# Attention scores of a half head: three passes over 64 rows from unstacked queries and keys, in place of two passes over 128 rows from stacked ones

## The chip, the cores and the metric

The kernel runs on one core of one Trainium2 chip. The metric is the time of one execution on the device in microseconds (us). The kernel before took 1044.98 us, the median of three runs (1044.03 to 1045.5). All inputs and outputs lie in the chip's memory as float32.

## The reference, cut to what matters

One layer over 512 tokens of width 2048, with 16 learned meta tokens ahead of them (528 rows). A normalised input is multiplied by one matrix of 2048 x 8192. Its columns are the queries, keys, values and gates of 8 heads of retention and of 8 heads of differential attention, 128 columns a head each. A head of the attention has two half heads of 64 columns, with a softmax each. The outputs of all heads are normalised, gated and multiplied by a second matrix of 2048 x 2048, added to the input and normalised once more.

```python
def diff_attention(q, k, v, valid, lam):          # q, k: (B, L, H, 2, 64), v: (B, L, H, 128)
    ...
        s = jnp.einsum('bqhcd,bkhcd->bhcqk', qb, k).astype(jnp.float32) * scale
        s = jnp.where(allowed[None, None, None], s + bias[None, :, None], -jnp.inf)
        p = jax.nn.softmax(s, axis=-1)
        a = p[:, :, 0] - lam * p[:, :, 1]
        return jnp.einsum('bhqk,bkhe->bqhe', a.astype(v.dtype), v)
```

The change touches how `s` is computed: for each half head `c`, the product of a block of 128 queries with the keys they may see, a sum over 64 numbers.

## The kernel before, in words

The kernel keeps float32 accuracy on a matrix engine that takes a shorter format (`F32R` in the code): each operand is split into a high part, rounded to that format, and a low part, the rest. A product of two such operands is then three products: high by high, high by low, low by high. The fourth, low by low, is left out.

The program goes through the 8 heads. For each, `project` makes eight projections one after the other (`rv rq rk rg dv dq dk dg`; in the last head the four of the attention come first). A projection is 16 blocks of 128 rows of the contraction times three products, so 48 products of 512 columns, or 96 of 264 columns where the 16 meta tokens are needed too (names ending in `v` and `k`). Its weights come from memory in pieces of 512 KB. ScalarE rounds each piece (`wh`, line 104) and VectorE subtracts (`wl`, line 105).

The attention and retention of a head are generators, `ret_task` and `diff_task`. They are advanced by `step` between the pieces of the projections, so that their small products stand among the next projections' large ones. The exact place of each instruction on its engine is set by the tile framework's scheduler, which simulates a time line while the program is built and orders each engine's queue by it; engines then run their queues in that order.

The steps that the change touches, all for one head `h` of the attention:

- After projection `dq` (lines 712 to 722) the queries, 128 partitions by 512 tokens in PSUM, are written to SBUF. Half head `s` holds partitions 64 s to 64 s + 63. Before, each half head gets its own tile of 128 partitions, the high part in the upper 64 and the low part in the lower 64: one ScalarE and one VectorE instruction a half head.
- After projection `dk` (lines 723 to 735) each half head's keys are written as two tiles of 128 partitions, [high; high] and [low; low]. For each half head and each of the two PSUM tiles of 264 columns these are two ScalarE and two VectorE instructions over 64 partitions.
- In `diff_task` (lines 555 to 597) there are four blocks of 128 queries, `b` = 0 to 3, which see 144, 272, 400 and 528 keys. For each half head the scores are two products over 128 rows: [q high; q low] by [k high; k high], and by [k low; k low]. (This includes low by low.) For `b` = 3 the 528 keys are two parts of 264 columns, so four products. The scores sit in PSUM tiles `s_d`: three buffers shared with other small products (`pm`) for `b` < 3, one double buffer (`pd`) for `b` = 3. VectorE adds the distance term and takes the row's maximum (line 584), ScalarE takes the exponential (line 587). The two softmaxes are combined, transposed (line 608) and multiplied by the values.

A stacked operand uses all 128 rows of the matrix engine though the contraction has only 64.

Of the kernel before, what the change touches and what calls it, by code (L numbers as in the profile page):

```python
# [28 lines left out]
# |o| beyond OMAX squares past float32. Squares are of o / 2; QMAX is the mean of 128 of them at which  # L29
# the sum of o * o passes float32 (its 1/sqrt is then 0)  # L30
# [6 lines left out]
def hymba_kernel(ctx: ExitStack, tc: tile.TileContext, x, meta, norm_g, w_in, w_out, g_ret, g_diff,  # L37
# [12 lines left out]
    def f(t):  # L50
        return t.bitcast(F32)
# [10 lines left out]
    # ---------------- weight pieces: 1024 columns of a partition at a time, split into hi and lo  # L62
    # in the last head the attention goes before the retention, whose way to the output is shorter
# [12 lines left out]
    for n0, nw in chunks:  # L76
        n = 1024 // nw
        # the last head's two outputs come last
        for ks in pairs if n0 == 0 else [slice(k, k + n) for k in range(0, KT, n)]:
            pieces.append((w_out_t[:, ks, n0:n0 + nw], nw))  # L80
# [6 lines left out]
    def load_raw(upto):  # L87
        for i in range(len(raws), min(upto, len(pieces))):
            src, nw = pieces[i]
            if i == 3:  # L90
                # one more buffer than the others have: the gates' of the attention
                raws[i] = [ap.tile([P, SEQ], F32, tag=t, name=f"wr{i}_{t}") for t in ("sgr", "sgd")]
                for j, r in enumerate(raws[i]):
                    nc.sync.dma_start(out=r.rearrange("p (k n) -> p k n", n=nw),
                                      in_=src[:, j * 4:j * 4 + 4, :])
                continue
            r = wp.tile([P, 1024], F32, tag="wr", name=f"wr{i}")
            nc.sync.dma_start(out=r.rearrange("p (k n) -> p k n", n=nw), in_=src)
            raws[i] = [r[:, :512], r[:, 512:]]
            if i >= 4:  # L100
                raws[i] = [r]
# [5 lines left out]
    def place(i):  # L107
        """Buffers of a piece's hi and lo, in as many parts as it is split in."""
        nw = pieces[i][1]
        if i < 2 or i == len(pieces) - 4:  # L110
            # the first projection's pieces, and one of the last four, sit in buffers of the attention
            parts = [(ap.tile([P, 512], F32R, tag="r2k", bufs=4, name=f"wh{i}_{j}"),
                      ap.tile([P, 512], F32R, tag=("vh", "vl")[i % 2], bufs=2, name=f"wl{i}_{j}")) for j in range(2)]
        elif i == 2:
            parts = [[ap.tile([P, L], F32R, tag=f"{t}{j}", name=f"w{i}_{t}{j}")[:, :512] for t in ("dkh", "dkl")]
                     for j in range(2)]
        else:
            hi, lo = (wp.tile([P, 1024], F32R, tag=t, name=f"{t}{i}") for t in ("wh", "wl"))
            n = 1024 // len(raws[i])
            parts = [(hi[:, j:j + n], lo[:, j:j + n]) for j in range(0, 1024, n)]  # L120
        kp = 1024 // nw // len(parts)
        views = [[t.rearrange("p (k n) -> p k n", n=nw) for t in p] for p in parts]
        loaded[i] = lambda k: [t[:, k % kp, :] for t in views[k // kp]]
        return parts
# [17 lines left out]
    # ---------------- inputs, constants  # L142
    xt = big.tile([P, 4, D], F32, tag="mix", name="xt")
    # the meta tokens' rows in quarters: partition 16 q + t holds columns 512 q .. of row t
# [31 lines left out]
    # adds the four quarters of each row of the meta tokens  # L176
# [3 lines left out]
    # ---------------- u = rms_norm(h) transposed, split  # L180
# [3 lines left out]
    def rsqrt_rows(r, n, nm):  # L184
        """r: sums of D squares per row -> 1/sqrt(mean + EPS)."""
        pool.tensor_scalar(r[:n], r[:n], 1.0 / D, EPS, op0=ALU.mult, op1=ALU.add)
        pool.tensor_tensor(out=r[:n], in0=r[:n], in1=mhalf[:n, 0:1], op=ALU.pow)
# [5 lines left out]
    def row_squares(j, c0, c1, eng):  # L193
        """Sums of squares of some columns of 128 tokens."""
        t = xt[:, j, c0 * P:c1 * P]
        jk = ap.tile([P, 1024], BF16, tag=("p2", "p2", "dq0", "dq1")[j], bufs=2 if j < 2 else 1, name=f"jk_x{j}_{c0}")[:, :(c1 - c0) * P]
        to = parts_x[j][:, used[j]:used[j] + 1]
        used[j] += 1
        if eng is act:
            act.activation(jk, t, AF.Square, accum_out=to)  # L200
        else:
            vec.tensor_tensor_reduce(jk, t, t, op0=ALU.mult, op1=ALU.add, scale=1.0, scalar=0.0, accum_out=to)
# [18 lines left out]
    def warm(n):  # L221
        """The tensor engine's clock rises only under load: keep it busy until there is work."""
# [32 lines left out]
    def turn(i, s, j):  # L255
        """Two 128-column blocks of 128 tokens' rows, transposed."""
# [27 lines left out]
    def first_two():  # L284
        """The first value and query projections, in step with the arrival of the tokens and the weights."""
# [8 lines left out]
        def run(i, half, s, which):  # L294
            """Products of two blocks of 128 of a projection's contraction."""
# [114 lines left out]
    # lambda: exp(lq1.lk1) - exp(lq2.lk2) + lam_init, negated, on every partition  # L410
# [12 lines left out]
    # tiles of 16 keys go through the tensor engine once: [hi; hi; lo] against [hi; lo; hi], 32 partitions apart  # L423
# [13 lines left out]
    # ---------------- attention tasks; each yield lets projection products go in between  # L437
    mix = {"f": big.tile([P, 2 * HEADS, SEQ], F32, tag="mix", name="mixf")}

    def finish(po, col, T, gate, nm):  # L440
        oc = ap.tile([P, L], F32, tag="s2k", bufs=4, name=f"oc_{nm}")[:, :SEQ]
        vec.tensor_scalar(oc, po, OMAX, -OMAX, op0=ALU.min, op1=ALU.max)
        # squares of both halves of the partitions summed, then [hi; lo] of them over the partitions
# [9 lines left out]
        # mean squares along one row -> over the partitions -> 1/sqrt -> back along a row, on every partition  # L453
# [20 lines left out]
    def v_rows(vT, nm, centre):  # L474
# [4 lines left out]
        # retention: key tiles of 128 from the first meta token, 16 keys last  # L479
        # attention: the meta tokens' tile last, then full tiles of tokens  # L480
# [74 lines left out]
    def diff_task(h, T):  # L555
# [3 lines left out]
        qs = T["dq"]  # L559
        ks = T["dk"]  # L560
        aa = []
        for b in range(4):
            w = 2 * 72 + P * b
            zz = sm.tile([P, 2], F32, tag="zz", name=f"zz_{nm}_{b}")
            pp = []
            for s in range(2):
                if b < 3:
                    sp = pm(f"s_{nm}_{b}_{s}")[:, :w]
                    for i in range(2):
                        pe.matmul(sp, qs[s][:, b * P:(b + 1) * P], ks[s][i][:, :w], start=i == 0, stop=i == 1)  # L570
                    shape = lambda t: t
                else:
                    sp = pd(f"s_{nm}_{b}_{s}")[:, :, :HL]
                    for i in range(2):
                        for q in range(2):
                            pe.matmul(sp[:, q, :], qs[s][:, b * P:(b + 1) * P], ks[s][i][:, q * HL:(q + 1) * HL],  # L576
                                      start=i == 0, stop=i == 1)
# [20 lines left out]
        # A transposed: (rows, key column, first query, columns) per tile; the products follow one step behind  # L598
# [31 lines left out]
    # ---------------- projections  # L630
# [42 lines left out]
    def early_mix():  # L673
        """The first heads' outputs, split while the last projection runs."""
# [6 lines left out]
    for h in range(HEADS):  # L681
        T = {}
        for name in order[h]:
# [28 lines left out]
            elif name == "dq":  # L712
                # each half head's queries as [hi; lo] over the partitions, scaled by powers of two
                (o, a, b), = outs
                c = DH ** -0.5 * 2.0 ** (h + 1)
                T[name] = []
                for s in range(2):
                    t = ap.tile([P, SEQ], F32R, tag=f"dq{s}", name=f"{nm}_{s}")
                    src = o[s * DH:(s + 1) * DH]
                    act.activation(t[:DH], src, AF.Copy, scale=c)  # L720
                    vec.scalar_tensor_tensor(t[DH:], src, c, f(t[:DH]), op0=ALU.mult, op1=ALU.subtract)
                    T[name].append(t)
            else:
                # each half head's keys as [hi; hi] and [lo; lo]
                T[name] = []
                for s in range(2):
                    t1 = ap.tile([P, L], F32R, tag=f"dkh{s}", name=f"{nm}h_{s}")
                    t2 = ap.tile([P, L], F32R, tag=f"dkl{s}", name=f"{nm}l_{s}")
                    for o, a, b in outs:
                        src = o[s * DH:(s + 1) * DH]  # L730
                        act.copy(out=t1[:DH, a:b], in_=src)
                        act.copy(out=t1[DH:, a:b], in_=src)
                        vec.tensor_tensor(out=t2[:DH, a:b], in0=src, in1=f(t1[:DH, a:b]), op=ALU.subtract)
                        vec.tensor_tensor(out=t2[DH:, a:b], in0=src, in1=f(t1[DH:, a:b]), op=ALU.subtract)
                    T[name].append((t1, t2))
# [8 lines left out]
    # ---------------- output projection, residual, final norm  # L744
# [13 lines left out]
    for ci, (n0, nw) in enumerate(chunks):  # L758
# [21 lines left out]
        def evac(t):  # L780
            # rows so far, their squares' sums, and the rows times the final gain
# [36 lines left out]
        else:  # L818
            prefetch(pi + np_)
            wt = [loaded.pop(pi + i) for i in range(np_)]  # L820
            for t in range(4):
# [6 lines left out]
                # the last rows in more parts: nothing else is left for their way out to hide behind  # L828
# [11 lines left out]
def tables():  # L840
    """Constants of the shapes: -|q - k| with the chunk mask, and each head's decay g ** |t - s| with its mask."""
# [55 lines left out]
```

## Time and profile before

| | |
|---|---|
| Median of three runs | 1044.98 us |
| Profiled execution, first to last instruction (span) | 1049.9 us |
| TensorE: matmul busy, share, instructions | 1029.7 us, 98%, 6423 |
| TensorE: weight loads busy | 926.3 us, 88% |
| VectorE busy | 511.4 us, 49% |
| ScalarE busy | 448.1 us, 43% |
| Mean granted TensorE clock | 0.993 |

The profile is one execution, whose span is 4.9 us above the median of the timed runs. PE is the matmul side of TensorE, PEld its weight loads, DVE is VectorE, ACT ScalarE, POOL GpSimd, SP the engine whose queue issues most DMAs. Matmuls are pipelined, so the duration of one is its way through the array; what it costs in a row of matmuls is the distance from its start to the next one's start, called its slot here. A weight load normally starts as the matmul before it starts.

### The profile page before, as it was taken

Reading aid. Unit: us, or ns where it says so; the run is one execution under the profiler, and the core shown is the slowest. Engines: PE = TensorE matmul, PEld = TensorE weight load, DVE = VectorE, ACT = ScalarE, POOL = GpSimd, SP = SyncE. Lnnn points to the kernel's source line nnn. Section 1 sums busy time; section 2 is a strip of 40 time slices with the busy share of each in tenths; the row PEclk is TensorE's granted clock in tenths of the full one; section 3 lists DMA queues with packets and bytes.
Section 4 is the critical chain, followed back from the end, with each engine's and each line's share of the span. In section 5 each row is a group of like instructions: output and inputs, shape, how many; then the busy total and the mean of one; then the engine's idle time right before and its main releaser. Section 6 shows DMA issues by size and latency. Waiting matters only on the chain.

```text
span 1049.9 us, 15748 instructions
## 1 busy us (share of the span) xinstructions
PE 1029.7 (98%) x6423; PEld 926.3 (88%) x6423; DVE 511.4 (49%) x1012; ACT 448.1 (43%) x814; POOL 48.0 (5%) x96
## 2 busy tenths in 40 slices
PE   6999999999999999999999999999999999899996
PEld 6999998999899989998999899989899888788896
DVE  6553544454445444645463536353637462344342
ACT  6443544363436343634363436343636452232232
POOL 3200000000000000000000000000000000000001
PEclk8999999999999999999999999999999999999999
DMA  9323332342233223322433233323332314373324
GB/s 282 92 83 102 93 87 81 83 110 82 81 87 107 81 81 96 97 83 79 102 91 93 68 103 90 101 61 103 91 101 69 103 61 130 92 261 100 101 61 160
DMA packets 156312, 105.70 MB, mean 101 GB/s; under 512 B 8320, under 2 KB 143632, under 8 KB 155728
## 3 DMA queue, kind: packets, MB, share of 16 engines
q1 hardware_dynamic: 155632, 102.86, 34.1%
q10 hardware_dynamic: 576, 1.84, 0.5%
q8 instruction: 50, 0.82, 0.3%
q14 instruction: 22, 0.18, 0.1%
q0 software_dynamic: 32, 0.01, 0.0%
HBM read 100.43 MB, written 4.23 MB: 100 GB/s over the span
## 4 chain that ended last, share of the span: by engine, by line
PE 94%; DMA 3%; ACT 1%; DVE 1%; POOL 1%; issue 0%; SPq 0%; POOLq 0%
PE pj_dv L282 9%; PE pj_rk L282 9%; PE pj_dk L282 9%; PE pj_rv L282 9%; PE pj_dg L282 9%; PE pj_dq L282 9%; PE pj_rg L282 9%; PE pj_rq L282 9%; PE y L511 5%; PE y L509 4%; PE y L510 4%; PE s_d L570 1%; PE at_d L608 1%; PE s_d L576 1%; DMA xt<-in_x_dram 1%; PE ut L262 1%
## 5 line engine op out<-in xcount | busy, mean ns | idle before, releaser
L104 ACT CAST wh<-wr 128x1024 fp32r<-128x1024 f32 (+1 forms) x157 | 163.2, 1041 | 321.7 <-issue 117.4
L105 DVE TENSOR_TENSOR wl<-wr,wh 128x1024 fp32r<-128x1024 f32 (+1 forms) x157 | 190.8, 1217 | 218.8 <-ACT wh L104 218.2
L509 PE MATMUL y<-wh,mh 128*128 128x512 f32 (+1 forms) x260 | 90.4, 349 | 2.8 <-ACT mh L670 2.8
L511 PE MATMUL y<-wh,ml 128*128 128x512 f32 (+1 forms) x260 | 90.8, 351 | 0.0
L510 PE MATMUL y<-wl,mh 128*128 128x512 f32 (+1 forms) x260 | 90.7, 349 | 0.0
L509 PEld LDWEIGHTS y<-wh,mh 128*128 128x128 f32 x260 | 49.6, 191 | 9.4 <-ACT mh L670 3.2
L282 PE MATMUL pj_rk<-uh,wh 128*128 128x264 f32 x256 | 56.3, 288 | 0.0
L282 PE MATMUL pj_rk<-uh,wl 128*128 128x264 f32 x256 | 55.6, 285 | 0.0
L282 PE MATMUL pj_rk<-ul,wh 128*128 128x264 f32 x256 | 55.5, 284 | 0.0
L511 PEld LDWEIGHTS y<-wh,ml 128*128 128x128 f32 x260 | 49.7, 191 | 6.2
L510 PEld LDWEIGHTS y<-wl,mh 128*128 128x128 f32 x260 | 49.5, 191 | 6.1
L282 PE MATMUL pj_dv<-uh,wh 128*128 128x264 f32 x256 | 54.3, 286 | 0.0
L587 ACT ACTIVATE p_d<-p_d,mx_d 128x144 f32<-128x144 f32 (+3 forms) x64 | 36.6, 572 | 40.5 <-DVE mx_d L586 39.3
L282 PE MATMUL pj_rv<-uh,wh 128*128 128x264 f32 x256 | 53.3, 287 | 0.3
L282 PE MATMUL pj_rv<-uh,wl 128*128 128x264 f32 x256 | 53.3, 286 | 0.0
L282 PE MATMUL pj_rv<-ul,wh 128*128 128x264 f32 x256 | 52.8, 285 | 0.0
L282 PE MATMUL pj_dv<-uh,wl 128*128 128x264 f32 x256 | 52.6, 286 | 0.0
L282 PE MATMUL pj_dk<-uh,wh 128*128 128x264 f32 x256 | 52.3, 286 | 0.0
L282 PE MATMUL pj_dv<-ul,wh 128*128 128x264 f32 x256 | 52.1, 285 | 0.0
L282 PE MATMUL pj_dk<-uh,wl 128*128 128x264 f32 x256 | 52.0, 285 | 0.0
L282 PE MATMUL pj_dk<-ul,wh 128*128 128x264 f32 x256 | 51.9, 284 | 0.0
L282 PE MATMUL pj_dq<-uh,wh 128*128 128x512 f32 x128 | 51.2, 400 | 0.0
(402 smaller groups left out, 2445.9 us busy)
## 6 DMA issues: line engine op xcount, KB each, us to landing
wr<-in_w_in_dram SPq DMA_DIRECT2D x127, 512.0 KB, 4.2
wr<-in_w_out_dram SPq DMA_DIRECT2D x32, 512.0 KB, 3.9
xt<-in_x_dram SPq DMA_DIRECT2D x8, 512.0 KB, 7.0
hr<-in_x_dram SPq DMA_DIRECT2D x4, 1024.0 KB, 8.3
tab<-in_decay_tab_dram SPq DMA_DIRECT2D x8, 288.0 KB, 2.8
bc_r<-rd_r SPq DMA_DIRECT2D x8, 256.0 KB, 4.1
bc_d<-rd_d SPq DMA_DIRECT2D x8, 256.0 KB, 4.6
out_dram<-hr ACTq DMA_DIRECT2D x4, 448.0 KB, 3.8
```

The source lines that it names most:

```text
L104: act.copy(out=hi, in_=raw)
L105: eng.tensor_tensor(out=lo, in0=raw, in1=f(hi), op=ALU.subtract)
L262: pe.transpose(groups[i, s][:, k, j * P:(j + 1) * P], xt[:, 2 * i + j, c * P:(c + 1) * P], ident)
L282: pe.matmul(o, w_, u_[:, kt, a:b], start=first, stop=last)
L509: pe.matmul(o, ah, bh, start=start, stop=False)
L510: pe.matmul(o, ah, bl, start=False, stop=False)
L511: pe.matmul(o, al, bh, start=False, stop=stop)
L570: pe.matmul(sp, qs[s][:, b * P:(b + 1) * P], ks[s][i][:, :w], start=i == 0, stop=i == 1)
L576: pe.matmul(sp[:, q, :], qs[s][:, b * P:(b + 1) * P], ks[s][i][:, q * HL:(q + 1) * HL], start=i == 0, stop=i == 1)
L587: act.activation(p, p, AF.Exp, bias=mx, scale=slope, accum_out=zz[:, s:s + 1])
L608: pe.transpose(at[:n, b * P - q0:(b + 1) * P - q0], aa[b][:, kc:kc + n], ident)
```

## The change

The queries and keys are no longer stacked. `dq` is written as one high and one low tile of 128 partitions by 512, `dk` as one high and one low tile of 128 by 528; half head 0 is partitions 0 to 63 of each, half head 1 partitions 64 to 127. A half head's scores are three products over its own 64 partitions (high by high, high by low, low by high) instead of two over 128. The program marks such a product as one for half of the array's rows, the first half for half head 0, the second for half head 1. For `b` < 3 the code asks for both half heads' products in turn, one of each; for `b` = 3 it asks for the six products of one half head and then, after a `yield`, for the six of the other.

```diff
-        qs = T["dq"]
-        ks = T["dk"]
...
+            def operands(s):
+
+                rows = slice(s * DH, s * DH + DH)
+                qh, ql = (t[rows, b * P:(b + 1) * P] for t in T["dq"])
+                kh, kl = (t[rows] for t in T["dk"])
+                return (qh, kh), (qh, kl), (ql, kh)
+
+            if b < 3:
+                sps = [pm(f"s_{nm}_{b}_{s}")[:, :w] for s in range(2)]
+                for i in range(3):
+                    for s in range(2):
+                        q_, k_ = operands(s)[i]
+                        pe.matmul(sps[s], q_, k_[:, :w], start=i == 0, stop=i == 2)
             for s in range(2):
                 if b < 3:
-                    sp = pm(f"s_{nm}_{b}_{s}")[:, :w]
-                    for i in range(2):
-                        pe.matmul(sp, qs[s][:, b * P:(b + 1) * P], ks[s][i][:, :w], start=i == 0, stop=i == 1)
+                    sp = sps[s]
                     shape = lambda t: t
                 else:
                     sp = pd(f"s_{nm}_{b}_{s}")[:, :, :HL]
-                    for i in range(2):
-                        for q in range(2):
-                            pe.matmul(sp[:, q, :], qs[s][:, b * P:(b + 1) * P], ks[s][i][:, q * HL:(q + 1) * HL],
-                                      start=i == 0, stop=i == 1)
+                    for q in range(2):
+                        for i, (q_, k_) in enumerate(operands(s)):
+                            pe.matmul(sp[:, q, :], q_, k_[:, q * HL:(q + 1) * HL], start=i == 0, stop=i == 2)
...
                 (o, a, b), = outs
                 c = DH ** -0.5 * 2.0 ** (h + 1)
-                T[name] = []
-                for s in range(2):
-                    t = ap.tile([P, SEQ], F32R, tag=f"dq{s}", name=f"{nm}_{s}")
-                    src = o[s * DH:(s + 1) * DH]
-                    act.activation(t[:DH], src, AF.Copy, scale=c)
-                    vec.scalar_tensor_tensor(t[DH:], src, c, f(t[:DH]), op0=ALU.mult, op1=ALU.subtract)
-                    T[name].append(t)
+                hi, lo = (ap.tile([P, SEQ], F32R, tag=f"dq{i}", name=f"{nm}_{i}") for i in range(2))
+                act.activation(hi, o, AF.Copy, scale=c)
+                vec.scalar_tensor_tensor(lo, o, c, f(hi), op0=ALU.mult, op1=ALU.subtract)
+                T[name] = (hi, lo)
             else:
-                T[name] = []
-                for s in range(2):
-                    t1 = ap.tile([P, L], F32R, tag=f"dkh{s}", name=f"{nm}h_{s}")
-                    t2 = ap.tile([P, L], F32R, tag=f"dkl{s}", name=f"{nm}l_{s}")
-                    for o, a, b in outs:
-                        src = o[s * DH:(s + 1) * DH]
-                        act.copy(out=t1[:DH, a:b], in_=src)
-                        act.copy(out=t1[DH:, a:b], in_=src)
-                        vec.tensor_tensor(out=t2[:DH, a:b], in0=src, in1=f(t1[:DH, a:b]), op=ALU.subtract)
-                        vec.tensor_tensor(out=t2[DH:, a:b], in0=src, in1=f(t1[DH:, a:b]), op=ALU.subtract)
-                    T[name].append((t1, t2))
+                hi, lo = (ap.tile([P, L], F32R, tag=f"dk{t}0", name=f"{nm}{t}") for t in "hl")
+                for o, a, b in outs:
+                    act.copy(out=hi[:, a:b], in_=o)
+                    vec.tensor_tensor(out=lo[:, a:b], in0=o, in1=f(hi[:, a:b]), op=ALU.subtract)
+                T[name] = (hi, lo)
```

Lines after the change stand about 10 further down in `diff_task`: the score products are lines 577 and 586 (570 and 576 before). The rows of the built programs below have the scheduler's order. `s_d_1_0` is the score tile of block `b` = 1, half head 0. Before, `dq_0` and `dq_1` are the stacked queries of half heads 0 and 1; after, `dq_0` is the high tile of both half heads and `dq_1` the low one. Numbers at the ends of names count buffers.

PE in head 0, blocks 0 and 1, among the products of projection `dg`, before:

```order
L570 MATMUL s_d_0_0_1257<-dk0l_1213,dq_0_1083 128x144
L282 MATMUL pj_dg_0_1278<-uh,wl_1161 128x512
L282 MATMUL pj_dg_0_1278<-uh,wh_1160 128x512
L570 MATMUL s_d_0_1_1265<-dk0h_1222,dq_1_1086 128x144
L570 MATMUL s_d_1_0_1312<-dk0h_1212,dq_0_1083 128x272
L282 MATMUL pj_dg_0_1278<-ul,wh_1160 128x512
L570 MATMUL s_d_1_0_1312<-dk0l_1213,dq_0_1083 128x272
```

and after:

```order
L577 MATMUL s_d_0_0_1241<-dk0h,dq_0_1083 128x144
L577 MATMUL s_d_0_1_1242<-dk0h,dq_0_1083 128x144
L282 MATMUL pj_dg_0_1264<-ul,wh_1101 128x512
L282 MATMUL pj_dg_0_1264<-uh,wl_1102 128x512
L577 MATMUL s_d_1_0_1298<-dk0h,dq_0_1083 128x272
L282 MATMUL pj_dg_0_1264<-uh,wh_1158 128x512
L577 MATMUL s_d_0_0_1241<-dk0l,dq_0_1083 128x144
L577 MATMUL s_d_0_1_1242<-dk0l,dq_0_1083 128x144
L577 MATMUL s_d_0_0_1241<-dk0h,dq_1_1084 128x144
L577 MATMUL s_d_0_1_1242<-dk0h,dq_1_1084 128x144
L577 MATMUL s_d_1_0_1298<-dk0l,dq_0_1083 128x272
L577 MATMUL s_d_1_0_1298<-dk0h,dq_1_1084 128x272
```

The six products of block 0 now stand as three pairs, one product of each half head; block 1's first half head stands unpaired, and products over 128 rows (`pj_dg`) come between.

PE in head 0, block 2, before:

```order
L282 MATMUL pj_rv_0_1387<-uh,wl_1282 128x264
L570 MATMUL s_d_2_0_1366<-dk0h_1212,dq_0_1083 128x400
L570 MATMUL s_d_2_0_1366<-dk0l_1213,dq_0_1083 128x400
L570 MATMUL s_d_2_1_1374<-dk0h_1222,dq_1_1086 128x400
L570 MATMUL s_d_2_1_1374<-dk0l_1223,dq_1_1086 128x400
L282 MATMUL pj_rv_1_1388<-uh,wl_1282 128x264
```

and after:

```order
L577 MATMUL s_d_2_0_1354<-dk0h,dq_0_1083 128x400
L577 MATMUL s_d_2_1_1355<-dk0h,dq_0_1083 128x400
L577 MATMUL s_d_2_0_1354<-dk0l,dq_0_1083 128x400
L577 MATMUL s_d_2_1_1355<-dk0l,dq_0_1083 128x400
L577 MATMUL s_d_2_0_1354<-dk0h,dq_1_1084 128x400
L577 MATMUL s_d_2_1_1355<-dk0h,dq_1_1084 128x400
```

Four products of one kind became three pairs with nothing between them. Block 3 is, in each half head, a row of six products of that half head (four before).

DVE in head 0, from the first key instruction to the first score instruction, before:

```order
L733 TENSOR_TENSOR dk0l_0_1213<-pj_dk0_0_1099,dk0h_0_1212 64x264
L734 TENSOR_TENSOR dk0l_0_1213<-pj_dk0_0_1099,dk0h_0_1212 64x264
L471 TENSOR_TENSOR oc_r0_1089<-oc_r0_1089,bc_r0_1241 128x512
L733 TENSOR_TENSOR dk0l_0_1213<-pj_dk0_1_1100,dk0h_0_1212 64x264
L734 TENSOR_TENSOR dk0l_0_1213<-pj_dk0_1_1100,dk0h_0_1212 64x264
L501 TENSOR_TENSOR vl_d0_1245<-vp_d0_1243,vh_d0_1244 128x512
L472 SCALAR_TENSOR_TENSOR mixf_625<-oc_r0_1089,gcol_94,sg_rg0_860 128x512
L733 TENSOR_TENSOR dk0l_1_1223<-pj_dk0_0_1099,dk0h_1_1222 64x264
L734 TENSOR_TENSOR dk0l_1_1223<-pj_dk0_0_1099,dk0h_1_1222 64x264
L733 TENSOR_TENSOR dk0l_1_1223<-pj_dk0_1_1100,dk0h_1_1222 64x264
L734 TENSOR_TENSOR dk0l_1_1223<-pj_dk0_1_1100,dk0h_1_1222 64x264
L505 TENSOR_TENSOR v_std_618<-vp_d0_1243,v_std_618 16x128
```

and after:

```order
L733 TENSOR_TENSOR dk0l_1211<-pj_dk0_0_1097,dk0h_1210 128x264
L733 TENSOR_TENSOR dk0l_1211<-pj_dk0_1_1098,dk0h_1210 128x264
L471 TENSOR_TENSOR oc_r0_1087<-oc_r0_1087,bc_r0_1225 128x512
L501 TENSOR_TENSOR vl_d0_1229<-vp_d0_1227,vh_d0_1228 128x512
L472 SCALAR_TENSOR_TENSOR mixf_625<-oc_r0_1087,gcol_94,sg_rg0_860 128x512
L505 TENSOR_TENSOR v_std_618<-vp_d0_1227,v_std_618 16x128
```

All the low keys are now made ahead of line 471, which waits for a DMA; before, three quarters of them stood behind it.

## Rows read from the trace of the kernel before

**Rows 1.** The page: busy time by engine, the granted clock, the chain.

```profile
PE 1029.7 (98%) x6423; PEld 926.3 (88%) x6423; DVE 511.4 (49%) x1012; ACT 448.1 (43%) x814; POOL 48.0 (5%) x96
...
PEclk8999999999999999999999999999999999999999
...
PE 94%; DMA 3%; ACT 1%; DVE 1%; POOL 1%; issue 0%; SPq 0%; POOLq 0%
```

**Rows 2.** Waits of PE, the one behind start-up: line, waited for, us, times, longest.

```profile
PE y L509 <- ACT mh L670: 2.8, 1, 2.8
```

**Rows 3.** Time line of PE: start, duration, instruction; a product of 144 columns.

```profile
117.64 0.40 PE L282 MATMUL pj_dg<-ul,wh 128*128 128x512 f32 x1
117.87 0.23 PE L570 MATMUL s_d<-dk0h,dq 128*128 128x144 f32 x1
...
118.22 0.39 PE L282 MATMUL pj_dg<-uh,wh 128*128 128x512 f32 x1
```

**Rows 4.** Time line of PE: products of 400 and 264 columns.

```profile
125.96 0.34 PE L570 MATMUL s_d<-dk0h,dq 128*128 128x400 f32 x1
...
126.68 0.28 PE L282 MATMUL pj_rv<-uh,wl 128*128 128x264 f32 x1
...
131.18 0.41 PE L576 MATMUL s_d<-dk0h,dq 128*128 128x264 f32 x2
...
131.67 0.28 PE L282 MATMUL pj_rv<-uh,wh 128*128 128x264 f32 x1
```

**Rows 5.** Time line of PE and PEld, from 64-row products to 128-row ones, start-up.

```profile
6.84 0.19 PE L234 MATMUL first<-part_m,sel 64*64 64x1 f32 x1
6.97 0.14 PEld L224 LDWEIGHTS idle<-ident 128*128 128x128 f32 x1
7.13 0.38 PE L224 MATMUL idle<-ident 128*128 128x128 f32 x2
...
11.07 0.53 PE L242 MATMUL first<-ident,mt 64*128 64x64 f32 x3
11.29 0.31 PE L242 MATMUL first<-ident,mt 64*128 64x64 f32 x1
11.53 0.29 PEld L224 LDWEIGHTS idle<-ident 128*128 128x128 f32 x2
11.80 0.64 PE L224 MATMUL idle<-ident 128*128 128x128 f32 x2
12.02 0.63 PE L224 MATMUL idle<-ident 128*128 128x128 f32 x2
```

**Rows 6.** Stretches of the same start-up; the clock stands after POOL's column.

```profile
5.50:8.80 3.30, 0.96 (x7) 0.50 (x5) 0.84 (x3) 1.05 (x2) 0.74 (x2) 1.00 0.93 323
9.00:15.00 6.00, 4.09 (x20) 3.83 (x21) 3.30 (x10) 4.99 (x9) 1.67 (x4) 0.50 1.05 291
```

**Rows 7.** Time line of PE and PEld: weights of 16 columns between ones of 128.

```profile
143.35 0.39 PE L282 MATMUL pj_rq<-uh,wl 128*128 128x512 f32 x1
143.35 0.42 PEld L608 LDWEIGHTS at_d<-ident,p_d 128*16 128x16 f32 x3
143.58 0.49 PE L608 MATMUL at_d<-ident,p_d 128*16 128x128 f32 x3
144.14 0.40 PE L282 MATMUL pj_rq<-ul,wh 128*128 128x512 f32 x1
```

**Rows 8.** Key and query instructions of ACT and DVE, 96 to 125 us.

```profile
L731 ACT CAST dk0h<-pj_dk 64x264 fp32r<-64x264 f32 x4 | 1.5, 373 | 3.6 <-DVE dk0l L734 3.4
L720 ACT ACTIVATE dq<-pj_dq 64x512 fp32r<-64x512 f32 x2 | 1.2, 586 | 1.5 <-DVE dq L721 1.5
L500 ACT CAST vh_d<-vp_d 128x512 fp32r<-128x512 f32 x1 | 0.6, 587 | 0.0
L734 DVE TENSOR_TENSOR dk0l<-pj_dk,dk0h 64x264 fp32r<-64x264 f32 x4 | 1.7, 431 | 0.1
```

**Rows 9.** Who waited for line 734, the low keys: us in total, times.

```profile
  PEld s_d L570: 1.4, 4
```

## The prediction

> **What bounds the kernel now.** First the page: PE is busy for 1029.7 of 1049.9 us and the chain that ends last is 94% PE, with the granted clock high almost throughout; DVE and ACT are under half busy [rows 1]. Then the waits of PE: behind the start-up there is one of note, 2.8 us near the end [rows 2]. So time is the number of PE's instructions times the distance from one start to the next (a slot), and I read slots from the time line.
>
> Three slots matter. A product of 512 columns takes 0.23 us (117.64 to 117.87). One of 144 columns and one of 512 behind it take 0.35 together (117.87 to 118.22), so the short one costs 0.12, though its columns alone would be 144/512 of 0.23, or 0.065 [rows 3]. I take 0.116 for it, and read it as a floor: what the load of the next 128-column weights takes. Products of 400 columns take 0.18 (four in 0.72), those of 264 take 0.122 (four in 0.49) [rows 4]; 272 columns lie just above, 0.125.
>
> **The score products, taken as a plain row.** Before, a head has four products each of 144, 272 and 400 columns and eight of 264: 4 x 0.116 + 4 x 0.125 + 4 x 0.18 + 8 x 0.122 = 2.66 us. The change makes six, six, six and twelve of them with the same columns, half as many again: +1.33 a head, +10.6 us over eight. Half the rows do not make a product shorter: at start-up the 64-row products of 64 columns stand 0.11 apart and the 128-row ones of 128 columns 0.21 (11.07 to 11.29 is two slots, 11.80 to 12.02 one) [rows 5], so columns set the slot.
>
> **What pairs give back.** Where two half heads stand next to each other, the two halves of the array could work at once. The order has this for block 0 and block 2 of seven heads, three pairs each. In the last head no two neighbours are of different halves; blocks 1 and 3 have no such pairs anywhere, and block 3 alone holds twelve of a head's thirty products. No row shows two such products. From one side: nothing overlaps, +10.6. From the other: a pair takes one product's slot, weights included, so blocks 0 and 2 save 3 x 0.116 + 3 x 0.18 = 0.89 us a head, 6.2 over seven heads, and +4.4 is left. I take the middle course that the floor suggests: the streams overlap but the weight loads, one a product, still follow each other at 0.116. Then pairs of 144 gain nothing, and a pair of 400 costs 0.232 in place of 0.36: 3 x 0.128 x 7 = 2.7 back, so +7.9.
>
> **Going from 128 rows to 64 and back.** The 240 products of the new scores stand in 58 stretches between 128-row work: seven in each of heads 0 to 6, nine in the last. That is 116 changes. The start-up shows the step back from 64 rows, twice. Normally a weight load starts as the matmul before it starts. Here the last 64-row product starts at 11.29 and the next weights, of 128 rows, only at 11.53; nothing is named that they wait for. From 11.29 to the start of the second 128-row product at 11.80 is 0.51, where two undisturbed slots are 0.11 + 0.21, so the step costs 0.19 [rows 5]. That stretch ran at half the clock, 0.50, so at 1.2 of the 2.4 GHz [rows 6]; if the cost is one of cycles it is 0.095 at the full clock. The other step fell at the full clock: from 6.84 to 7.13 is 0.29 for two short products, whose two slots are at most 0.23, so at least 0.06 [rows 5, 6]. I take 0.10 for a step back. The step into 64 rows stands behind semaphore waits in both places and cannot be read. It could cost nothing; the nearest row is the step back, so I take 0.10 for it too. 116 x 0.10 = 11.6 us. Bounds: 0 (below zero is excluded, since a weight load that starts early is already hidden) and 116 x 0.19 = 22.0.
>
> The Trainium skill (TensorEngine Tiling (Array Packing), Key Properties) says that a change of the tiling mode, not merely of the tile, drains TensorE; it gives no price. The start-up rows agree with it. Other rows do not go so far: weights of 16 columns start loading with the 512-column matmul ahead of them (both 143.35), and from 143.58 the three 16-column products and the 512-column one behind them take 0.56 us, which is 3 x 0.11 + 0.23 [rows 7], so a change of columns costs nothing. If rows went as columns do, the term would be 0 and the sum 11.6 lower, the second rival below.
>
> **ACT and DVE.** The queries' and keys' instructions fall from ten to three on each engine per head. On ACT 2 x 0.586 + 8 x 0.373 = 4.2 us become some 0.59 + 2 x 0.37 = 1.3, since 128 partitions cost what 64 do (0.587 beside 0.586) [rows 8]. DVE's eight subtractions of 0.431 [rows 8] become two, and its second query instruction goes. That is over 20 us on each engine, all beside PE's work, so worth nothing but for waits that PE has on them. Those are 1.4 us: four times the load of a score product's weights waited for the low keys [rows 9]. In the new order all low keys stand ahead of DVE's wait for a DMA, so I take the 1.4 off (bounds 1.4 and 0). Next due after them is the score bank that block 1's second half needs; 19 products, 4.4 us, stand ahead of it, while DVE has less queued than before. The wait at the end [rows 2] stays: PE's order from the last attention head on is unchanged.
>
> **Sum.** 7.9 + 11.6 - 1.4 = +18.1 us. The profiled execution's 1049.9 becomes 1068.0. It lies 4.9 above the median of the runs, which the page does not explain; the same addition on 1044.98 gives 1063.1.
>
> **Rivals.**
> - Dearer steps: a drain is a fixed time and costs 0.19 at the full clock as well. 7.9 + 22.0 - 1.4 = +28.5, so 1073.5, and 1076 if pairs overlap nothing. For it: the half-clock row is the cleaner of the two. Against: the full-clock row's 0.06 to 0.10.
> - Free steps: row groups change as freely as column groups. 7.9 - 1.4 = +6.5, so 1051.5; 1048 to 1054 with the pairs' bounds. For it: rows 7. Against: the late weight loads of rows 5, which nothing else explains.
> - Not slower: the halves run as two separate arrays, weights and all, with no drain. The place is the pairs. A product of 144 columns then costs its columns, 0.065, and a pair as much as one: block 0 saves 6 x 0.116 - 3 x 0.065 = 0.50 a head, block 2 saves 0.54, together 7.3 over seven heads, so +3.3, and with the waits +1.9: 1046.9. It decides once a pair of 144 costs less than one weight load's 0.116. The Trainium skill (the same page and section) speaks for it: tiles can load weights and multiply in parallel. No row here shows it. Against it: blocks 1 and 3 cost 0.75 + 1.46 us a head in place of 0.50 + 0.98, so the unpaired eighteen of thirty products lose 0.74 a head whatever the pairs do.
>
> **How the numbers follow.** Forecast 0.55, dearer steps 0.16, free steps 0.20, not slower 0.09. Within 0.2%, 2.1 us, is about what a measurement of this kernel cannot tell from no change. Only the last rival lies there (1046.9): 0.07 for the same, and 0.02 of it plus 0.01 of luck at the wait near the end for faster; the rest, 0.90, is slower. The range from 1048 to 1076 holds the forecast with its bounds, free steps and most of dearer steps; the forecast's own range is 1056 to 1070.
>
> **What would show it.** In the profile after: the first weight load of a stretch of 64 rows, and the first of 128 rows behind it, start well after the matmul ahead of them started (0.1 to 0.25 us) instead of with it. A pair of 400 columns takes 0.23 from pair to pair, not 0.36 or 0.18. Six products of block 3 take 0.73 plus the two steps. The waits of score weights for the low keys are gone. ACT and DVE are some 20 us less busy each, with no effect. What would make the prediction wrong: weight loads that keep starting with the matmul ahead (free steps), or a new wait of PE for a score bank or a rounded weight piece.

## The result, and the profile after

The changed kernel takes 1070.78 us, the median of four runs (1070.38 to 1071.82), beside 1045.24 for the kernel before (four runs): a ratio of 1.0248, with an interval of 1.0234 to 1.0263. So it is 25.5 us slower. The prediction was +18.1, that is 1063 with a range of 1048 to 1076. The direction and the terms were right, two sizes were not, and their errors ran against each other. The time lies just outside the forecast's own range (1056 to 1070) and nearer to the rival of dearer steps (1073.5).

The page after, the lines that answer to [rows 1]: busy time by engine, the granted clock, the chain.

```profile
PE 1053.0 (98%) x6503; PEld 930.4 (87%) x6503; DVE 484.4 (45%) x956; ACT 425.0 (40%) x758; POOL 47.4 (4%) x96
...
PEclk8999999999999999999999999999999999999998
...
PE 96%; DMA 2%; ACT 1%; DVE 1%; issue 0%; SPq 0%; POOL 0%; POOLq 0%
```

PE has 80 instructions more and 23.3 us more of busy time. DVE lost 27.0 us and ACT 23.1, without a gain in time. TensorE still sets the end, at the same clock.

The waits of PE after, all that the view lists (waited for, us, times, longest):

```profile
PE first L242 <- DVE mt L239: 3.8, 1, 3.8
PE idle L224 <- POOL ident masks.py:199: 2.6, 1, 2.6
PE ut L262 <- DVE xt L215: 1.5, 1, 1.5
PE first L234 <- DVE part_m L230: 0.9, 1, 0.9
```

All four are at start-up, so no new wait explains the loss. The wait of [rows 2] is not there, and none of the other eight profiles shows it, so it seems to belong to the one execution that was profiled before and not to the kernel. In that trace PE then ran on at a lower clock, as two of its stretches show (us, busy time by engine, and the clock behind POOL's column):

```profile
916.00:919.50 3.50, 0.68 (x4) 0.38 (x3) 1.88 (x3) 1.09 (x2) 0.00 (x0) 1.00 0.34 117
919.50:924.00 4.50, 4.50 (x15) 3.55 (x14) 1.48 (x2) 0.48 (x1) 0.00 (x0) 0.62 0.69 249
```

PE stood for 2.8 us, and the 4.5 us behind it held 15 matmuls at a mean clock of 0.62, where a later profile of nearly the same program (`before_pool_copy` below) has 22 in the same stretch at 1.00. Seven slots of 0.23 are 1.6 us, and with the 2.8 that makes 4.4. The 4.9 us by which that span was said to lie above the median compares two different things: in every run on record a span is 1.7 to 1.9 us shorter than the time of the same execution (after, 1070.1 beside 1071.82). If that holds there too, the profiled execution took some 6.7 us more than the median, and 2.3 of them stay unexplained.

So the loss is to be looked for in the score products. Their time line on PE after: block 2 of head 0 (126.62 to 128.03), then the first half of block 3 (from 133.40).

```profile
126.62 0.40 PE L282 MATMUL pj_dg<-uh,wl 128*128 128x512 f32 x1
126.94 0.45 PE L577 MATMUL s_d<-dk0h,dq 64*128 64x400 f32 x2
127.23 0.34 PE L577 MATMUL s_d<-dk0l,dq 64*128 64x400 f32 x2
127.41 0.34 PE L577 MATMUL s_d<-dk0h,dq 64*128 64x400 f32 x2
127.69 0.51 PE L282 MATMUL pj_rv<-uh,wh 128*128 128x264 f32 x2
128.03 0.40 PE L282 MATMUL pj_rv<-ul,wh 128*128 128x264 f32 x2
...
133.40 0.40 PE L282 MATMUL pj_rv<-uh,wl 128*128 128x264 f32 x2
133.73 0.39 PE L586 MATMUL s_d<-dk0h,dq 64*128 64x264 f32 x1
133.96 0.28 PE L586 MATMUL s_d<-dk0l,dq 64*128 64x264 f32 x1
134.08 0.41 PE L586 MATMUL s_d<-dk0h,dq 64*128 64x264 f32 x2
134.33 0.28 PE L586 MATMUL s_d<-dk0l,dq 64*128 64x264 f32 x1
134.45 0.28 PE L586 MATMUL s_d<-dk0h,dq 64*128 64x264 f32 x1
134.66 0.51 PE L282 MATMUL pj_rv<-uh,wh 128*128 128x264 f32 x2
```

And the weight loads of the same places:

```profile
126.94 0.19 PEld L577 LDWEIGHTS s_d<-dk0h,dq 64*128 64x128 f32 x2 [0.36 <-DVE mx_d L595]
127.05 0.19 PEld L577 LDWEIGHTS s_d<-dk0l,dq 64*128 64x128 f32 x2
...
133.28 0.31 PEld L282 LDWEIGHTS pj_rv<-uh,wl 128*128 128x128 f32 x2
133.73 0.18 PEld L586 LDWEIGHTS s_d<-dk0h,dq 64*128 64x128 f32 x1
133.84 0.19 PEld L586 LDWEIGHTS s_d<-dk0l,dq 64*128 64x128 f32 x1
...
134.65 0.30 PEld L282 LDWEIGHTS pj_rv<-uh,wh 128*128 128x128 f32 x2
```

Three things are to be seen.

**A pair costs one product.** In block 2 an x2 row is one product of each half head, and the two start together (0.003 us apart in the trace). From 127.23 to 127.41 the pair takes 0.18, the slot of one product of 400 columns [rows 4]. The weight loads come in twos as well.

**Inside a stretch the columns set the slot.** In block 3, from 133.96 to 134.45, four products take 0.49, so 0.122 each, as before.

**Each step costs about 0.2, in two parts.** In block 2 the slots are: 512 columns to the first pair 0.32 (0.23 undisturbed), first pair to second 0.29 (0.18), last pair to the next 128-row product 0.28 (0.18), two products of 264 columns behind it 0.34 (0.24). That is 0.09 + 0.11 for the step in and 0.10 + 0.10 for the step out, 0.40 for the stretch. The loads say why there are two parts. Normally a load starts one product ahead of its own; here the first load of a stretch starts with its own product (133.73 and 133.73; 134.65 and 134.66). First the load is late, then its product is 0.11 longer (0.39 beside 0.28), about the distance of two loads (133.73 to 133.84): the load that is otherwise hidden seems to lie inside it. A stretch that is one pair of 144 columns costs less, 0.34 in the trace.

Added up over all stretches of the trace, from the start of the matmul ahead to the start of the second one behind, less the slots of the 128-row matmuls in between, the score products cost 23.0 us before and 47.7 after: +24.7, beside +25.5 in the medians. What is left, 0.8, is less than the 1.4 to 1.8 us by which runs of one kernel differ.

The key and query instructions of ACT and DVE that answer to [rows 8], 96 to 125 us:

```profile
L732 ACT CAST dk0h<-pj_dk 128x264 fp32r<-128x264 f32 x2 | 0.7, 377 | 0.0
L726 ACT ACTIVATE dq<-pj_dq 128x512 fp32r<-128x512 f32 x1 | 0.6, 582 | 0.0
L733 DVE TENSOR_TENSOR dk0l<-pj_dk,dk0h 128x264 fp32r<-128x264 f32 x2 | 0.8, 423 | 0.0
```

They cost what was forecast (128 partitions as much as 64), and nothing waits for line 733 any more, where [rows 9] had 1.4 us.

### The profile page after: what moved, and what is told of

Its sections match the earlier page's. It is cut to its first block, busy times and chain, and to the rows that moved or that the text cites. A ratio compares the mean times of both kernels' runs of the same rounds, so it can differ in the third digit from the quotient of the medians.

```text
span 1070.1 us, 15771 instructions
## 1 busy us (share of the span) xinstructions
PE 1053.0 (98%) x6503; PEld 930.4 (87%) x6503; DVE 484.4 (45%) x956; ACT 425.0 (40%) x758; POOL 47.4 (4%) x96
## 4 chain that ended last, share of the span: by engine, by line
PE 96%; DMA 2%; ACT 1%; DVE 1%; issue 0%; SPq 0%; POOL 0%; POOLq 0%
PE pj_rv L282 9%; PE pj_dg L282 9%; PE pj_dv L282 9%; PE pj_rk L282 9%; PE pj_dk L282 9%; PE pj_rq L282 8%; PE pj_dq L282 8%; PE pj_rg L282 8%; PE y L509 5%; PE y L510 5%; PE y L511 5%; PE s_d L577 2%; PE s_d L586 1%; PE at_d L617 1%; DMA xt<-in_x_dram 1%; PE ut L262 1%
## 5 line engine op out<-in xcount | busy, mean ns | idle before, releaser
L282 PE MATMUL pj_dg<-ul,wh 128*128 128x512 f32 x128 | 52.3, 409 | 0.0
L282 PE MATMUL pj_dg<-uh,wh 128*128 128x512 f32 x128 | 51.9, 406 | 0.0
```

What stands on the lines that cost most here:

```text
L282: pe.matmul(o, w_, u_[:, kt, a:b], start=first, stop=last)
```

## The experiments

The theory was: the row change costs 0.195 a step, the pairs overlap fully, and the third pass costs its columns. Ratios are to the kernel before, with its own runs beside.

**pad128: three passes, but over 128 rows.** The changed kernel, but each half head has key tiles of its own, its keys in 64 partitions and zeros in the other 64. No step and no pair is left.

```diff
-                rows = slice(s * DH, s * DH + DH)
-                qh, ql = (t[rows, b * P:(b + 1) * P] for t in T["dq"])
-                kh, kl = (t[rows] for t in T["dk"])
+                qh, ql = (t[:, b * P:(b + 1) * P] for t in T["dq"])
+                kh, kl = T["dk"][s]
...
```

> The changed kernel's three passes and its thirty score products a head, but over all 128 rows: a half head's keys lie in a tile whose other 64 partitions are zero, so queries need no slicing and no product is a half-array one. Theory (the cost is the step between 128-row and 64-row work, 0.39 us for the two steps of each of 58 stretches, and pairs of half-array products run fully side by side): the steps' 22.6 us go, the pairs' 6.2 us are lost; against the kernel before +10.6 for the products and -1.5 for the waits, so about 1054. Rival A (the cost is the number of products and weight loads, or the order the scheduler makes of them): as the changed kernel, about 1070. Rival B (a half-array product is itself slower than a full one): between the two, nearer 1054, with stretches of block 3 at 0.73 us like theory's; A and theory differ by 16 us.

Measured: 1055.38 us (1054.27 to 1055.94) beside 1044.23, ratio 1.0095 [1.0071, 1.0119]. The six products of block 3 on PE:

```profile
132.20 0.41 PE L282 MATMUL pj_rv<-uh,wl 128*128 128x264 f32 x2
132.44 0.29 PE L585 MATMUL s_d<-kph,dq 128*128 128x264 f32 x1
...
133.04 0.28 PE L585 MATMUL s_d<-kph,dq 128*128 128x264 f32 x1
133.16 0.41 PE L282 MATMUL pj_rv<-uh,wh 128*128 128x264 f32 x2
```

They take 0.72 (132.44 to 133.16) with nothing at either end; the same six over 64 rows take 1.13 with their two steps (0.73 + 0.40). All score products cost 31.8 us in the trace, about what their slots alone add up to (8 x 3.99 = 31.9). That is 8.8 more than before: the 10.6 of the third pass, less 1.8 of waits that the kernel before has on top of its slots. (The medians say 11.2 and the ratio 9.9, with an interval of 7.4 to 12.4; what the second tile of keys costs elsewhere was not looked for.) So three passes without pairs and steps are some 15 us faster than the changed kernel, and the steps must cost about that more than the pairs give back.

**no_pairs: half head by half head in the code.** The changed kernel, but blocks 0 to 2 ask for the three products of half head 0 and then those of half head 1.

```diff
-                for i in range(3):
-                    for s in range(2):
+                for s in range(2):
+                    for i in range(3):
```

> The changed kernel with the two loops over passes and half heads swapped, so that the three products of one half head follow each other and then the other's; the stretches stay 58. Theory (neighbours of different halves overlap fully, weights too): the three pairs of block 2 become a row of six with one overlap at most in the middle, 5 or 6 x 0.18 in place of 3 x 0.18, and block 0 loses one or two slots of 0.11 of its three pairs: +0.47 to +0.76 a head in seven heads, so +3.3 to +5.3, about 1075. Rival (weight loads follow each other at 0.116, as the prediction took it): +0.38 x 7 = +2.7 at most in block 2 and nothing in block 0. Rival (no overlap that matters): the same time as the changed kernel, 1070.8.

Measured: 1070.52 us (1070.22 to 1071.42), ratio 1.0245 [1.0225, 1.0265]: the same as the changed kernel. The theory (about 1075) missed, and the first rival's cost, up to 2.7, does not show. The second rival has the number but not the reason, since the pairs are there. The order of block 0's last four products in the built program was

```
s_d0_0_0 <- dk0l, dq0_0      half head 0
s_d0_0_0 <- dk0h, dq0_1      half head 0
s_d0_0_1 <- dk0l, dq0_0      half head 1
s_d0_0_1 <- dk0h, dq0_1      half head 1
```

and what ran, on PE, first those four, then block 2:

```profile
118.59 0.34 PE L577 MATMUL s_d<-dk0l,dq 64*128 64x144 f32 x2
118.77 0.28 PE L577 MATMUL s_d<-dk0h,dq 64*128 64x144 f32 x2
118.88 0.33 PE L577 MATMUL s_d<-dk0l,dq 64*128 64x272 f32 x1
...
125.57 0.46 PE L577 MATMUL s_d<-dk0h,dq 64*128 64x400 f32 x2
125.86 0.35 PE L577 MATMUL s_d<-dk0l,dq 64*128 64x400 f32 x2
126.03 0.35 PE L577 MATMUL s_d<-dk0h,dq 64*128 64x400 f32 x2
126.32 0.39 PE L282 MATMUL pj_rv<-uh,wh 128*128 128x264 f32 x1
```

The two low-key products started together, though one of the high keys stood between them in the program; block 2 shows the same pairs as the changed kernel, 0.17 to 0.18 apart. So the order inside a stretch does not decide: the halves run side by side. No stage of the build makes the pairs: in the compiled program, too, PE's instructions for block 2 are three products over the first half of the rows and then three over the second, each behind its weight load, in all seven heads where they share a stretch. So PE started products of the second half ahead of products of the first that stand before them in its queue. The sentence ahead of the prediction, that engines run their queues in the scheduler's order, does not hold for the two halves of the array here; within a half the order is kept. The second half starts 0.010 us behind the first in block 2 and 0.006 in block 0, where its first product stood three and two places behind, and 0.003 in the changed kernel, where it stood one behind. The run therefore tells nothing of the price of a pair; that comes from block3_paired.

**step_rows64 and step_rows128: steps alone.** The kernel before, with 62 products of zero weights and 64 columns put between projection products, over 64 rows (the first edit, against the kernel before) or over 128 (the second, against the first). The making of the zero weights `zw` is left out.

```diff
...
+                if keys and kt % 8 == 4:
+                    pe.matmul(outs[0][:128, :64], zw[:64, :128], uh[:64, kt, :64], start=False, stop=False)
```

```diff
-                    pe.matmul(outs[0][:128, :64], zw[:64, :128], uh[:64, kt, :64], start=False, stop=False)
+                    pe.matmul(outs[0][:128, :64], zw[:128, :128], uh[:128, kt, :64], start=False, stop=False)
```

> The kernel before with 62 extra products, two in each projection of keys and values but the first, each 64 columns wide with all-zero weights of 64 rows and 128 columns, added into the projection's own sum, which they leave as it is. Theory (steps into and out of 64-row work cost 0.2 us each at the full clock): 62 x (0.11 + 0.34 to 0.39) = +28 to +31, about 1074. Rival A (more products only): 62 x 0.11 = +6.8, about 1052.

> The same 62 extra products at the same places, but with zero weights of 128 rows, so that no step is made. Theory and rival A alike: 62 x 0.11 = +6.8, about 1052. What tells them apart is the difference to the run with 64 rows: 21 to 24 us by the theory, 0 by rival A.

Measured: 1070.97 us (1070.7 to 1072.02), ratio 1.025 [1.0229, 1.027], over 64 rows, and 1051.71 (1051.13 to 1052.06), 1.0063 [1.0043, 1.0083], over 128. PE with one over 64 rows:

```profile
319.47 0.40 PE L282 MATMUL pj_dk<-uh,wl 128*128 128x264 f32 x2
319.81 0.29 PE L653 MATMUL pj_dk<-uh,zw 64*128 64x64 f32 x1
320.03 0.51 PE L282 MATMUL pj_dk<-uh,wh 128*128 128x264 f32 x2
320.38 0.40 PE L282 MATMUL pj_dk<-ul,wh 128*128 128x264 f32 x2
```

and with one over 128:

```profile
312.97 0.41 PE L282 MATMUL pj_dk<-uh,wl 128*128 128x264 f32 x2
313.21 0.19 PE L653 MATMUL pj_dk<-uh,zw 128*128 128x64 f32 x1
313.24 0.49 PE L282 MATMUL pj_dk<-uh,wh 128*128 128x264 f32 x2
313.56 0.41 PE L282 MATMUL pj_dk<-ul,wh 128*128 128x264 f32 x2
```

From row to row of two projection products there are 0.91 us in the first (319.47 to 320.38) and 0.59 in the second (312.97 to 313.56). The median over all 62 is 0.421 and 0.109 a product. The difference of the two kernels is 19.3 us, 0.31 for two steps. That is 2 to 5 us under the 21 to 24 that were expected: around a single product the unhidden load behind the step in (0.11) and the wait ahead of the step out (0.10) seem to be one and the same 0.11. The view shows no wait of these products for any engine, so a step alone makes the loads late; those of the score products need no wait for ACT or DVE either, although the view of the loads names DVE at some.

**step_cols64: the same with weights of 64 columns over 128 rows.** The edit is against step_rows128; the built program marks these products as ones for half of the array's columns.

```diff
-                    pe.matmul(outs[0][:128, :64], zw[:128, :128], uh[:128, kt, :64], start=False, stop=False)
+                    pe.matmul(outs[0][:64, :64], zw[:128, :64], uh[:128, kt, :64], start=False, stop=False)
```

> The 62 extra products of the two runs before at the same places, now with zero weights of 128 rows and 64 columns, so that the step is one of column groups and not of row groups. Theory (only a change of row groups drains; columns change freely, as the 16-column transposes before): at most what the 128-row products cost, +4 to +7, about 1050. Rival (any change of the tiling drains, at the price of the 64-row step): +27, about 1071.

Measured: 1051.92 us (1050.93 to 1052.58) beside 1045.06, ratio 1.0063 [1.0048, 1.0078], 0.111 a product. PE:

```profile
313.57 0.41 PE L282 MATMUL pj_dk<-uh,wl 128*128 128x264 f32 x2
313.81 0.19 PE L653 MATMUL pj_dk<-uh,zw 128*64 128x64 f32 x1
313.84 0.48 PE L282 MATMUL pj_dk<-uh,wh 128*128 128x264 f32 x2
314.17 0.40 PE L282 MATMUL pj_dk<-ul,wh 128*128 128x264 f32 x2
```

0.60 from row to row, where 128 rows and 128 columns had 0.59. Going to fewer columns of weights is free, as [rows 7] had it for 16; going to fewer rows is not.

**block3_paired: fewer stretches, more pairs.** The changed kernel, but block 3's twelve products in one stretch of six pairs instead of two stretches of six.

```diff
+            if b == 3:
+                sps = [pd(f"s_{nm}_{b}_0")[:, :, :HL], [pm(f"s_{nm}_{b}_1{q}")[:, :HL] for q in range(2)]]
+                part = [[sps[0][:, q, :] for q in range(2)], sps[1]]
+                for q in range(2):
+                    for i in range(3):
+                        for s in range(2):
+                            q_, k_ = operands(s)[i]
+                            pe.matmul(part[s][q], q_, k_[:, q * HL:(q + 1) * HL], start=i == 0, stop=i == 2)
...
```

> The changed kernel with block 3's twelve products asked for in one stretch of six pairs (half head 0 in the double bank, half head 1 in two of the small banks, its maximum taken in two parts), so 50 stretches in place of 58. Theory (0.39 us a stretch, a pair costs one product's slot): 8 x (0.39 + 6 x 0.122) = -9.0, about 1061.8. Rival (steps cost so, but in a pair weight loads follow each other at 0.116): 8 x (0.39 + 0.07) = -3.7, about 1067. Rival (a new wait of PE for the two small banks eats it): same as the changed kernel, 1070.8, with a wait of PE for DVE at the transposes or the scores.

Measured: 1062.81 us (1062.48 to 1063.1) beside 1045.06, ratio 1.0167 [1.0152, 1.0183]. PE:

```profile
133.05 0.40 PE L282 MATMUL pj_rv<-uh,wl 128*128 128x264 f32 x2
133.39 0.39 PE L585 MATMUL s_d<-dk0h,dq 64*128 64x264 f32 x2
...
134.11 0.28 PE L585 MATMUL s_d<-dk0h,dq 64*128 64x264 f32 x2
134.31 0.52 PE L282 MATMUL pj_rv<-uh,wh 128*128 128x264 f32 x2
```

Twelve products take 0.92 from the first to the next 128-row product (133.39 to 134.31), what six took in the changed kernel (133.73 to 134.66: 0.93). Eight stretches fewer at 1.13 are 9.0 us. The score products of the trace fell by 8.8, from 47.7 to 38.9, and the excess over the kernel before by 7.7, from 25.5 to 17.8 us. Weight loads that follow each other at 0.116 would have given 3.7. This settles the pairs: streams and weight loads both run side by side.

**before_pool_copy: the waits alone.** The kernel before, with the second copy of the low keys made by GpSimd, so that DVE has half as many key instructions.

```diff
-                        vec.tensor_tensor(out=t2[DH:, a:b], in0=src, in1=f(t1[DH:, a:b]), op=ALU.subtract)
+                        pool.tensor_copy(t2[DH:, a:b], f(t2[:DH, a:b]))
```

> The kernel before with one of the two copies of each half head's low keys made by the idle GpSimd engine from the other copy, in place of a second VectorE subtraction; scores still two stacked passes of 128 rows. Theory (the waits of score weights for the low keys, 1.4 us, and for VectorE's reading of the score banks, in all some 1.8 us, come of VectorE's queue there): up to -1.8, about 1043, which is at the edge of what can be told from no change. Rival (VectorE is held by its wait for a DMA in that place and not by its own work): no change, 1044 to 1045.

Measured: 1044.71 us beside 1045.06, ratio 0.9994 [0.9985, 1.0004]. In the trace the score products cost 21.2 us instead of 23.0, and the loads' waits for low keys, 1.4 us in [rows 9], come down to one line:

```profile
PEld s_d L570 <- POOL dk2l L734: 0.2, 1, 0.2
```

The runs do not show the 1.8 us: the interval reaches from 1.6 faster to 0.4 slower. How much of the waits comes back as time, or whether PE loses it again elsewhere, stays open; it is the smallest term.

No kernel here beats the one before clear of noise. By these numbers the best form of three passes would be, as an estimate, one stretch a head with pairs throughout: 3 x (0.116 + 0.125 + 0.18 + 2 x 0.122) + 0.39 = 2.39 us in place of 2.66, 2.2 us over eight heads. It needs all of a head's score tiles at once and was not tried.

## Why the prediction was right in its direction, and where its sizes were off

| term | predicted | measured, score products of the traces |
|---|---|---|
| third pass | +10.6 | +10.6 (pad128's +8.8 with the 1.8 of the waits put back) |
| pairs give back | -2.7 | -6.2 (one product a pair, as read and as block3_paired has it) |
| steps | +11.6 | +22.0 (what is left of the 47.7) |
| waits for low keys | -1.4 | -1.8 (not shown by the runs) |
| sum | +18.1 | +24.7 (25.5 in the medians) |

- **The bound.** Time as the number of PE's instructions times their slots, with pairs and steps counted in, accounts for all but 0.8 us; of 50 us less work on ACT and DVE nothing is seen in the time.
- **The third pass.** Right: columns set the slot and rows do not, as [rows 5] was read.
- **Pairs.** The step that failed is the middle course, "the streams overlap but the weight loads, one a product, still follow each other at 0.116". The loads of the two halves start together, and a pair costs one product: the bound of 6.2, not 2.7. The Trainium skill (TensorEngine Tiling (Array Packing), Key Properties) says that tiles load weights and multiply in parallel; these traces agree (0.18 from pair to pair of 400 columns). Loads side by side stood in the prediction as a bound and in the "not slower" rival, where they were joined to a pair of 144 columns at its columns' 0.065. That further saving did not come: in no_pairs a pair of 144 columns is followed 0.11 later (118.77 to 118.88), so at the floor of one product.
- **Steps.** The step that failed is "if the cost is one of cycles it is 0.095 at the full clock". [Rows 5] had 0.19 at half the clock, and at the full clock it is 0.19 to 0.20 as well: the 47.7 us less 25.7 of undisturbed slots (21.3 before, + 10.6 - 6.2) are 22.0, over 116 steps 0.19. So the total did not halve with the clock; the dearer-steps rival said so and was given 0.16. That it is a fixed time, as that rival had it, is not shown. The two parts differ: in the one row at half the clock the product starts 0.13 late and the next is 0.06 late behind it (11.29 to 11.53 less 0.11; 11.53 to 11.80 less 0.21), at the full clock the parts are 0.10 and 0.10 to 0.11, so the equal totals may be chance. The row that spoke against it, at least 0.06 and up to 0.10 at the full clock, was a lower bound from short products with floors of 0.11 in them. It was used as if it measured.
- **The signs named ahead.** The late first loads are there at both ends of a stretch, block 3 takes its 0.73 and two steps, and the waits for the low keys are gone. The pair of 400 columns was the one sign that failed: 0.18 from pair to pair, not 0.23.
- **That both steps cost alike,** which no row showed, was right: 0.09 + 0.11 in, 0.10 + 0.10 out.
- **The pairs in the last head.** There "no two neighbours are of different halves", and its three products of 400 columns stand alone, each half in a stretch of its own (0.93 us for three, as much as three pairs elsewhere). This held, but for the reason of stretches, not of neighbours, as no_pairs shows.
- **The profiled execution.** Its wait near the end and the low clock behind it explain 4.4 us of its excess, which was nearer to 6.7 than to the 4.9 of the prediction. "The wait at the end [rows 2] stays" was wrong, since no other profile lists one of PE there. The time forecast for the runs lost nothing by it, being the median plus a difference.

With 0.19 a step and full pairs the same working gives 10.6 - 6.2 + 22.0 - 1.4 = +25.0, that is 1070. That the number came out within 8 us is in part luck: one error took 10.4 too little for the steps, the other 3.5 too much for the pairs.

## What to carry to other kernels

By these numbers half-array products can pay only in long stretches: a stretch costs 0.31 to 0.39 us on top of its products, up to three undisturbed products of 264 columns, and pairs give one product's slot back each. So count the stretches between other work before the products. Work out a cost that one row shows at a lowered clock both as a time and as a number of cycles, and do not let a lower bound decide between the two. When a profiled execution is some us longer than the median, look for a wait that other profiles lack before any term is built on it, and compare a span with spans, not with times of the device.

## What the runs showed of the hardware that had not been expected

- Going from 128 rows to 64 or back cost 0.19 to 0.20 us a step at a granted clock of 1.00 (0.31 for both steps around a single product of 64 columns). The one step back that was read at 0.50 cost 0.19 [rows 5, 6], in other parts. Going to 64 columns of weights cost nothing (0.111 us a product beside 0.109).
- Products on the two halves of the array ran in pairs even where PE's queue had them one half after the other: starts 0.006 to 0.010 us apart, 1070.52 us beside 1070.78.
- The weight loads of the two halves also ran together, so twelve products in pairs took the 0.92 us of six.
